# Differential attention: each softmax's head on its own 64 rows of TensorE, three part products, three score buffers

## Chip, core and metric

The kernel runs on one core of a Trainium2 chip. The metric is the device time of one execution in microseconds; before the change it is 2722.09 us, the median of three runs (2720.32 to 2725.2).

## What is computed

An encoder trunk of two layers on 1024 tokens of width 1024, in float32. Layer 0 mixes tokens by differential attention: for each of 8 heads, two softmaxes over all 1024 keys, with queries and keys of 64 dimensions each, are subtracted and applied to values of 128 dimensions. Layer 1 uses windowed grouped attention. Each layer has a gated MLP with a short convolution, and an input embedding gated by a sigmoid. Only the first layer's attention is changed:

```python
def one_block(qb):
    s = jnp.einsum('bqhd,bkhd->bhqk', qb, k).astype(jnp.float32) * scale
    pr = jax.nn.softmax(s, axis=-1).reshape(B, H, 2, DIFF_Q_BLOCK, S)
    a = (pr[:, :, 0] - lam_full * pr[:, :, 1]).astype(v.dtype)
    return jnp.einsum('bhqk,bkhe->bqhe', a, v)
```

## The kernel before

Most products run in a one-pass float32 format of reduced precision. An operand is therefore split into a high and a low part, and a product of two operands is a sum of part products. Queries and keys lie in scratch memory as 64 high rows and 64 low rows per softmax head.

The stage of differential attention is `diff_attn`. Its units are (head h, block qt of 128 queries), 64 in all. For one unit, `weights` does this for each of the two softmaxes a: four score products (L784, L785) into a score buffer of 128 x 1024 (two PSUM banks, S0 or S1); the negated row maximum on VectorE (L786); the exponential with its row sum on ACT (L790) into one of 11 buffers `e`. A stacked tile holds high parts on rows 0 to 63 and low parts on rows 64 to 127; `k2` is the same key tile with the halves exchanged. So one product with `k1` gives high x high + low x low, and one with `k2` the two mixed terms: all four part products in two products of 128 rows. Then a reciprocal on VectorE (L799), and two instructions on POOL (L801, L802) scale the second exponential and add it to the first, which frees the second buffer.

`values` follows two units later (LAG = 2): eight transposes (L813) into banks b4 and b5, copied out by ACT (L817) and VectorE (L819); eight float32 products with the values (L822, sixteen passes in the trace) into b2 or b3; a copy and a square with row sum on ACT (L826, L828), which read the sum. After every fourth unit, `subln_steps` normalises four blocks: small instructions on VectorE (L726) and POOL (L729), four scalings (L734), four transposes (L740, b2 or b3), an eviction on ACT (L743).

The order of instructions on each engine isn't that of the code: a scheduler in the framework fills each engine's list by a timeline of its own when the program is built, and semaphores for the tiles follow from it. On the chip each engine takes its list strictly from the front.

The next stage, the output projection, starts when the transposed heads `oT` are there.

Of the kernel before, what the change touches and what calls it, by code (L numbers as in the profile page):

```python
# [7 lines left out]
F32 = mybir.dt.float32  # L8
F32R = mybir.dt.float32r
# [4 lines left out]
PSUM = bass.MemoryType.PSUM  # L14
DRAM = bass.MemoryType.DRAM

P = 128
S = 1024
D = 1024
KT = D // P  # L20
HS = 512
# [32 lines left out]
def f32(ap):  # L54
    return ap.bitcast(F32)
# [55 lines left out]
END_BANKS = ["b2", "b3"]  # L111
P_BANKS = ["b0", "b1", "b4", "b5", "b6", "b7"]
DOWN_BANKS = ["b0", "b1", "b2", "b4", "b6", "b7", "b3", "b5"]
MIX_BANKS = ["b4", "b2", "b5", "b3"]


class Trunk:
# [603 lines left out]
    def subln_steps(self, h, hf, st, psum):  # L721

        nc = self.nc
        on, ss, z2 = st
        c = slice(hf * 4, hf * 4 + 4)
# [12 lines left out]
        tp = self.bank(psum, END_BANKS)  # L738
# [9 lines left out]
    def diff_attn(self, ap, psum, side):  # L748
        nc = self.nc
        v = nc.vector  # L750
        self.oT = [None] * NH
        ld, outs = {}, {}

        def load(h):
            b, hh = h // 2, 2 * (h % 2)
            qq, k1, k2 = (
                ap.at(f"{n}{h % 2}", [P, 2, S], F32R, self.nm("stk")) for n in ("q", "k", "l")
            )
            self.stack(k1[:], self.ks[b][:], slice(hh, hh + 2))
            self.stack(qq[:], self.qs[b][:], slice(hh, hh + 2))  # L760
            self.stack(k2[:], self.ks[b][:], slice(hh, hh + 2), swap=True)
            vt = ap.pools["v"].tile([P, 8, P], F32, tag="v", bufs=2, name=self.nm("v"))
            nc.sync.dma_start(vt[:], self.vs[:, :, h * P : (h + 1) * P])
            ld[h] = (qq, k1, k2, vt)
# [7 lines left out]
        def weights(h, qt):  # L772
# [3 lines left out]
            qq, k1, k2, _ = ld[h]  # L776
            sm = self.cp.tile([P, 8], F32, tag="sm", bufs=8, name=self.nm("sm"))
            es = []
            for a in range(2):
                ps = psum.at(f"S{a}", [P, S], F32, self.nm("S"))  # L780
                q_ = qq[:, a, qt * P : (qt + 1) * P]
                for kb in range(2):
                    sl = slice(kb * HS, (kb + 1) * HS)
                    nc.tensor.matmul(ps[:, sl], q_, k1[:, a, sl], start=True, stop=False)  # L784
                    nc.tensor.matmul(ps[:, sl], q_, k2[:, a, sl], start=False, stop=True)  # L785
# [19 lines left out]
        def values(h, qt, ea):  # L805

            vt = ld[h][3]
            at = ap.pools["a"].tile([P, 8, P], F32, tag="a", bufs=ABUF, name=self.nm("aT"))
            for kh in range(2):
                tp = psum.at(f"b{4 + kh}", [P, 4, P], F32, self.nm("T"))  # L810
# [9 lines left out]
            acc = self.bank(psum, END_BANKS)  # L820
# [738 lines left out]
    def run(self, out):  # L1559
# [41 lines left out]
        with ExitStack() as c:  # L1601
            ap = self.attn_pools(c, "a0", ["k0", "q0", "l0", "v", "a", "k1", "q1", "l1", "e"])
            psum = Bank(c, self.tc, "ps_a0", ["S0", "b2", "b3", "b4", "b5", "S1"], PSUM)
            self.diff_attn(ap, psum, [])
# [76 lines left out]
```

## Time and profile before

| What | Value |
|---|---|
| median of three runs | 2722.09 us |
| profiled execution | 2722.41 us |
| its span | 2720.6 us |
| TensorE (PE) busy | 2631.9 us, 97% |
| VectorE (DVE) busy | 1935.3 us, 71% |
| ScalarE (ACT) busy | 1185.5 us, 44% |
| GpSimd (POOL) busy | 1109.1 us, 41% |
| mean granted TensorE clock | 0.991 |

A matmul's duration in the trace includes its way through the pipeline; how fast matmuls follow each other is read from their starts. PEld are the weight loads that lie beside them. A name such as `S<-stk,stk` is output and inputs.

### The profile page before, as it was taken

How to read it: one execution, taken by the hardware profiler on the slowest of the kernel's cores; microseconds unless marked ns; L12 is line 12 of the kernel's file. 1: busy time of each engine (PE TensorE's matmuls, PEld its weight loads, DVE VectorE, ACT ScalarE, POOL GpSimd, SP SyncE). 2: the span in 40 equal slices, each digit the busy share in tenths (PEclk: the TensorE clock that was granted, in tenths of full speed). 3: DMA queues.
4: the chain of work that ended last, by engine and by line, in shares of the span. 5: the costliest groups of instructions: out<-in, count | busy, mean ns of one | idle time of the engine just before them, and what ended most of it. 6: DMA issues, size and time to landing. Idle time of an engine off the chain costs nothing. (4 is left out here: it accounts for less than half of the span.)

```text
span 2720.6 us, 33379 instructions
## 1 busy us (share of the span) xinstructions
PE 2631.9 (97%) x12670; PEld 2187.4 (80%) x12670; DVE 1935.3 (71%) x2250; ACT 1185.5 (44%) x2090; POOL 1109.1 (41%) x625
## 2 busy tenths in 40 slices
PE   7999999999999999999999999999999999999998
PEld 6888888888788888878888788878778888788877
DVE  7650588884798888866677556873988888856664
ACT  5322577773444444441134326872544444421142
POOL 2642577774233434325312353442343444334211
PEclk9999999999999999999999999999999999999999
DMA  6443623302423232244314347104322223344122
GB/s 245 157 152 124 186 65 109 101 9 99 142 69 93 70 93 75 88 147 144 108 46 146 110 166 247 48 1 147 117 78 85 89 74 93 128 135 139 62 70 93
DMA packets 204133, 296.24 MB, mean 109 GB/s; under 512 B 9524, under 2 KB 138693, under 8 KB 200261
## 3 DMA queue, kind: packets, MB, share of 16 engines
q1 hardware_dynamic: 203349, 293.72, 33.2%
q8 instruction: 100, 1.64, 0.2%
q14 instruction: 60, 0.49, 0.1%
q10 hardware_dynamic: 624, 0.39, 0.1%
HBM read 207.83 MB, written 86.25 MB: 108 GB/s over the span
## 5 line engine op out<-in xcount | busy, mean ns | idle before, releaser
L152 POOL TENSOR_TENSOR wl<-wr,wh 128x1024 fp32r<-128x1024 f32 (+1 forms) x113 | 296.5, 2640 | 490.1 <-ACT wh L146 386.8
L1150 POOL TENSOR_TENSOR sf<-wr 128x1024 f32<-128x1024 f32 x44 | 146.9, 3338 | 503.1 <-DVE w L1160 503.1
L1325 DVE TENSOR_TENSOR res<-res,ps 128x512 f32<-128x512 f32 x320 | 216.8, 684 | 147.7 <-PE ps L245 145.0
L241 PE MATMUL ps<-gh,wh 128*128 128x512 f32 x704 | 275.4, 391 | 4.2 <-DVE ug L1266 3.2
L244 PE MATMUL ps<-gl,wh 128*128 128x512 f32 x704 | 275.1, 391 | 1.0 <-DVE gl L152 1.0
L245 PE MATMUL ps<-gh,wl 128*128 128x512 f32 x704 | 274.8, 390 | 0.0
L241 PE MATMUL ps<-hn,wh 128*128 128x512 f32 x544 | 215.2, 396 | 2.8 <-DVE gt L1423 1.9
L245 PE MATMUL ps<-hn,wl 128*128 128x512 f32 x544 | 213.5, 393 | 0.6 <-DVE wl L152 0.6
L244 PE MATMUL ps<-hn,wh 128*128 128x512 f32 x544 | 213.9, 393 | 0.0
L146 ACT CAST wh<-wr 128x1024 fp32r<-128x1024 f32 (+1 forms) x140 | 144.8, 1092 | 143.6 <-PE ps L244 95.8
L790 ACT ACTIVATE e<-S,sm 128x1024 f32<-128x1024 f32 x128 | 142.2, 1113 | 86.1 <-DVE sm L786 84.0
L146 ACT CAST gh<-gr 128x1024 fp32r<-128x1024 f32 x44 | 46.2, 1049 | 292.1 <-PE ps L245 213.3
L1159 ACT CAST w<-sf 128x1024 fp32r<-128x1024 f32 x88 | 92.7, 1053 | 184.4 <-PE ps L1188 108.9
L786 DVE TENSOR_REDUCE sm<-S 128x1 f32<-128x1024 f32 x128 | 152.2, 1216 | 17.1 <-PE S L785 15.6
L241 PEld LDWEIGHTS ps<-gh,wh 128*128 128x128 f32 x704 | 132.8, 189 | 32.7 <-ACT wh L146 3.5
L244 PEld LDWEIGHTS ps<-gl,wh 128*128 128x128 f32 x704 | 132.8, 189 | 29.2 <-DVE gl L152 1.7
L245 PEld LDWEIGHTS ps<-gh,wl 128*128 128x128 f32 x704 | 132.7, 189 | 27.7
L802 POOL TENSOR_TENSOR e<-e,e 128x1024 f32<-128x1024 f32 x64 | 152.0, 2375 | 5.2
L1186 PE MATMUL ps<-qb,w 128*128 128x512 f32 x352 | 137.3, 390 | 3.5 <-DVE uv L1262 3.5
L1186 PE MATMUL ps<-qa,w 128*128 128x512 f32 x352 | 136.7, 389 | 2.0 <-ACT w L1159 2.0
L1187 PE MATMUL ps<-qa,w 128*128 128x512 f32 x352 | 137.1, 389 | 0.0
L1187 PE MATMUL ps<-qb,w 128*128 128x512 f32 x352 | 137.0, 389 | 0.0
(256 smaller groups left out, 7255.2 us busy)
## 6 DMA issues: line engine op xcount, KB each, us to landing
wr<-ffn_w_up SPq DMA_DIRECT2D x88, 512.0 KB, 5.3
gs<-c SPq DMA_DIRECT2D x44, 512.0 KB, 3.0
wr<-ffn_w_down SPq DMA_DIRECT2D x22, 1024.0 KB, 5.1
gr<-gs SPq DMA_DIRECT2D x44, 512.0 KB, 4.3
qs<-rhl SPq DMA_DIRECT2D x32, 512.0 KB, 3.2
wr<-diff_w_qkv SPq DMA_DIRECT2D x12, 1024.0 KB, 5.8
ks<-rhl SPq DMA_DIRECT2D x20, 512.0 KB, 3.1
spill<-res SPq DMA_DIRECT2D x16, 512.0 KB, 3.0
```

What stands on the lines that cost most here:

```text
L146: self.nc.scalar.copy(out, in_)
L152: self.marks[eng] = eng.tensor_tensor(out, in_, f32(hi), op=ALU.subtract)
L241: ins = self.nc.tensor.matmul(out, ah, bh, start=first, stop=False)
L244: self.nc.tensor.matmul(out, ah, bl, start=False, stop=False)
L245: self.nc.tensor.matmul(out, al, bh, start=False, stop=last)
L786: v.tensor_reduce(sm[:, a : a + 1], ps[:], axis=AX.X, op=ALU.max, negate=True)
L790: nc.scalar.activation(e[:], ps[:], AF.Exp, bias=sm[:, a : a + 1], accum_out=sm[:, 2 + a : 3 + a])
L802: nc.gpsimd.tensor_tensor(ea[:], ea[:], eb[:], op=ALU.add)
L1150: eng.tensor_tensor(sf[:, 0:2], v[:, 2].unsqueeze(1).to_broadcast([P, 2, HS]), v[:, 0::3], op=ALU.add)
L1186: mm(ps, ah, bh, start=first and i == 0, stop=False, skip_group_check=True)
L1187: mm(ps, ah, bl, start=False, stop=False, skip_group_check=True)
L1325: v.tensor_tensor(self.res[dt][:, sl], self.res[dt][:, sl], acc[:], op=ALU.add)
```

## The change

The two softmaxes of a head now lie beside each other on the rows: the first on rows 0 to 63, the second on rows 64 to 127, for queries and for keys, with high and low parts behind each other in a partition. A score is the sum of three part products (high x high, high x low, low x high) of 64 rows each; low x low is left out. The code issues them in pairs, one for each softmax. The exchanged key tile and its loads are gone. There are three score buffers in turn (S0, S1, S2, six banks), and the banks b6 and b7 in turn hold all other tiles of the stage: transposes, value sums, and the transposes of `subln_steps`. In the program, each score product of 64 rows carries a tile size of 64 x 128 and the row position 0 or 64.

```diff
--- before.py
+++ after.py
@@ -111,6 +111,7 @@
 END_BANKS = ["b2", "b3"]
 P_BANKS = ["b0", "b1", "b4", "b5", "b6", "b7"]
 DOWN_BANKS = ["b0", "b1", "b2", "b4", "b6", "b7", "b3", "b5"]
+PAIR_BANKS = ["b6", "b7"]
 MIX_BANKS = ["b4", "b2", "b5", "b3"]
 
 
@@ -735,7 +736,7 @@
                 on[:, qt, :], on[:, qt, :], ss[:, qt : qt + 1], None, op0=ALU.mult
             )
         yield
-        tp = self.bank(psum, END_BANKS)
+        tp = self.bank(psum, PAIR_BANKS)
         for i in range(4):
             nc.tensor.transpose(
                 tp[:, i * P : (i + 1) * P], on[:, hf * 4 + i, :], self.ident
@@ -749,19 +750,20 @@
         nc = self.nc
         v = nc.vector
         self.oT = [None] * NH
-        ld, outs = {}, {}
+        ld, outs, turn = {}, {}, [0]
 
         def load(h):
             b, hh = h // 2, 2 * (h % 2)
-            qq, k1, k2 = (
-                ap.at(f"{n}{h % 2}", [P, 2, S], F32R, self.nm("stk")) for n in ("q", "k", "l")
-            )
-            self.stack(k1[:], self.ks[b][:], slice(hh, hh + 2))
-            self.stack(qq[:], self.qs[b][:], slice(hh, hh + 2))
-            self.stack(k2[:], self.ks[b][:], slice(hh, hh + 2), swap=True)
+            kk, qq = (ap.at(f"{n}{h % 2}", [P, 2, S], F32R, self.nm("stk")) for n in ("k", "q"))
+            for t, src in ((kk, self.ks[b]), (qq, self.qs[b])):
+                v_ = src[:].rearrange("(e r h) s -> r e h s", e=2, h=4)
+                for a in range(2):
+                    nc.sync.dma_start(
+                        f32(t[a * 64 : (a + 1) * 64]), v_[:, :, hh + a, :]
+                    )
             vt = ap.pools["v"].tile([P, 8, P], F32, tag="v", bufs=2, name=self.nm("v"))
             nc.sync.dma_start(vt[:], self.vs[:, :, h * P : (h + 1) * P])
-            ld[h] = (qq, k1, k2, vt)
+            ld[h] = (qq, kk, vt)
             self.rows_tile(self.oT, h, "oT")
             outs[h] = (
                 ap.pools["a"].tile([P, 8, P], F32, tag="o", bufs=2, name=self.nm("on")),
@@ -773,16 +775,24 @@
 
             if qt == 0:
                 load(h)
-            qq, k1, k2, _ = ld[h]
+            qq, kk, _ = ld[h]
             sm = self.cp.tile([P, 8], F32, tag="sm", bufs=8, name=self.nm("sm"))
+            qc = slice(qt * P, (qt + 1) * P)
+            ss = []
+            for _ in range(2):
+                ss.append(psum.at(f"S{turn[0] % 3}", [P, S], F32, self.nm("S")))
+                turn[0] += 1
+            for kb in range(2):
+                sl = slice(kb * HS, (kb + 1) * HS)
+                for i, (eq, ek) in enumerate(((0, 0), (0, 1), (1, 0))):
+                    for a in range(2):
+                        r = slice(a * 64, (a + 1) * 64)
+                        nc.tensor.matmul(
+                            ss[a][:, sl], qq[r, eq, qc], kk[r, ek, sl],
+                            start=(i == 0), stop=(i == 2),
+                        )
             es = []
-            for a in range(2):
-                ps = psum.at(f"S{a}", [P, S], F32, self.nm("S"))
-                q_ = qq[:, a, qt * P : (qt + 1) * P]
-                for kb in range(2):
-                    sl = slice(kb * HS, (kb + 1) * HS)
-                    nc.tensor.matmul(ps[:, sl], q_, k1[:, a, sl], start=True, stop=False)
-                    nc.tensor.matmul(ps[:, sl], q_, k2[:, a, sl], start=False, stop=True)
+            for a, ps in enumerate(ss):
                 v.tensor_reduce(
                     sm[:, a : a + 1], ps[:], axis=AX.X, op=ALU.max, negate=True
                 )
@@ -804,10 +814,10 @@
 
         def values(h, qt, ea):
 
-            vt = ld[h][3]
+            vt = ld[h][2]
             at = ap.pools["a"].tile([P, 8, P], F32, tag="a", bufs=ABUF, name=self.nm("aT"))
             for kh in range(2):
-                tp = psum.at(f"b{4 + kh}", [P, 4, P], F32, self.nm("T"))
+                tp = psum.cycle(PAIR_BANKS, [P, 4, P], F32, self.nm("T"))
                 for i in range(4):
                     kt = kh * 4 + i
                     nc.tensor.transpose(
@@ -817,7 +827,7 @@
                     nc.scalar.copy(at[:, 0:4], tp[:])
                 else:
                     v.tensor_copy(at[:, 4:8], tp[:])
-            acc = self.bank(psum, END_BANKS)
+            acc = self.bank(psum, PAIR_BANKS)
             for k in range(8):
                 nc.tensor.matmul(
                     acc[:, :P], at[:, k, :], vt[:, k, :], start=(k == 0), stop=(k == 7)
@@ -1599,8 +1609,8 @@
                 self.x_squares(i, tp.tile([P, D], F32, tag="t", name=self.nm("xsq")))
             self.qkv0(hn, self.xrcol, hp, tp, psum)
         with ExitStack() as c:
-            ap = self.attn_pools(c, "a0", ["k0", "q0", "l0", "v", "a", "k1", "q1", "l1", "e"])
-            psum = Bank(c, self.tc, "ps_a0", ["S0", "b2", "b3", "b4", "b5", "S1"], PSUM)
+            ap = self.attn_pools(c, "a0", ["k0", "q0", "v", "a", "k1", "q1", "e"])
+            psum = Bank(c, self.tc, "ps_a0", ["S0", "S1", "S2", "b6", "b7"], PSUM)
             self.diff_attn(ap, psum, [])
         gs = self.projected(0, io["diff_w_o"][0], pp[0])
         with ExitStack() as sc:
```

The scheduler places the work anew. At the start of the stage, on TensorE, before (S_251 and S_253 are the two softmaxes of unit 0, S_256 the first of unit 1):

```order
L784 MATMUL S_253_2204<-stk_243_2183,stk_242_2182 128x512
L785 MATMUL S_253_2204<-stk_244_2184,stk_242_2182 128x512
L784 MATMUL S_253_2204<-stk_243_2183,stk_242_2182 128x512
L785 MATMUL S_253_2204<-stk_244_2184,stk_242_2182 128x512
L784 MATMUL S_256_2218<-stk_243_2183,stk_242_2182 128x512
L785 MATMUL S_256_2218<-stk_244_2184,stk_242_2182 128x512
L784 MATMUL S_256_2218<-stk_243_2183,stk_242_2182 128x512
```

and now (S_250 and S_251 are the two softmaxes of unit 0, S_255 and S_256 those of unit 1, S_260 and S_261 of unit 2):

```order
L790 MATMUL S_250_2186<-stk_242_2173,stk_243_2174 128x512
L790 MATMUL S_251_2187<-stk_242_2173,stk_243_2174 128x512
L790 MATMUL S_250_2186<-stk_242_2173,stk_243_2174 128x512
L790 MATMUL S_251_2187<-stk_242_2173,stk_243_2174 128x512
L790 MATMUL S_255_2212<-stk_242_2173,stk_243_2174 128x512 x6
L790 MATMUL S_256_2213<-stk_242_2173,stk_243_2174 128x512 x6
L790 MATMUL S_260_2238<-stk_242_2173,stk_243_2174 128x512 x6
L790 MATMUL S_261_2239<-stk_242_2173,stk_243_2174 128x512 x6
L790 MATMUL S_270_2289<-stk_242_2173,stk_243_2174 128x512 x6
```

In unit 0 the products of the two softmaxes alternate, as in the code; from unit 1 on, all six of one softmax stand together, and all six of the other behind them.

In the middle of the stage, on TensorE, before (T_665 and T_666 are the transposes of unit 36, S_660 and S_662 the two softmaxes of unit 38):

```order
L784 MATMUL S_660_4081<-stk_592_3773,stk_591_3772 128x512
L785 MATMUL S_660_4081<-stk_593_3774,stk_591_3772 128x512
L784 MATMUL S_660_4081<-stk_592_3773,stk_591_3772 128x512
L785 MATMUL S_660_4081<-stk_593_3774,stk_591_3772 128x512
L822 MATMUL ps_657_4066<-v_594_3779,aT_654_4053 128x128 x8
L813 MATMUL T_665_4103<-identr_172,e_641_3991 128x128 x4
L813 MATMUL T_666_4109<-identr_172,e_641_3991 128x128 x4
L784 MATMUL S_662_4089<-stk_592_3773,stk_591_3772 128x512
L785 MATMUL S_662_4089<-stk_593_3774,stk_591_3772 128x512
L784 MATMUL S_662_4089<-stk_592_3773,stk_591_3772 128x512
L785 MATMUL S_662_4089<-stk_593_3774,stk_591_3772 128x512
```

and now (T_660 and T_661 are the transposes of unit 36, ps_662 its value sum, T_670 and T_671 are those of unit 37, S_743 and S_744 the softmaxes of unit 46, S_753 and S_754 of unit 47):

```order
L832 MATMUL ps_652_4204<-v_589_3893,aT_649_4191 128x128 x4
L790 MATMUL S_743_4662<-stk_675_4330,stk_676_4331 128x512 x6
L790 MATMUL S_744_4663<-stk_675_4330,stk_676_4331 128x512 x6
L832 MATMUL ps_652_4204<-v_589_3893,aT_649_4191 128x128 x4
L823 MATMUL T_660_4245<-identr_172,e_637_4130 128x128 x4
L823 MATMUL T_661_4251<-identr_172,e_637_4130 128x128 x4
L832 MATMUL ps_662_4257<-v_589_3893,aT_659_4244 128x128 x8
L823 MATMUL T_670_4300<-identr_172,e_647_4181 128x128 x4
L790 MATMUL S_753_4717<-stk_675_4330,stk_676_4331 128x512 x6
L790 MATMUL S_754_4718<-stk_675_4330,stk_676_4331 128x512 x6
L823 MATMUL T_671_4306<-identr_172,e_647_4181 128x128 x4
```

Scores were two to three units ahead of the transposes; now they are nine to ten units ahead, and the groups of six stand singly or in twos between transposes and values. The transposes and values of unit 36 follow each other with no score between.

On ACT at the same place, before (e_661 and e_663 are the exponentials of unit 38):

```order
L790 ACTIVATE e_661_4087,sm_659_4080<-S_660_4081,sm_659_4080 128x1024
L826 COPY on_595_3781<-ps_657_4066 128x128
L828 ACTIVATE jk_658_4076,ss_596_3782<-ps_657_4066 128x128
L817 COPY aT_664_4102<-T_665_4103 128x512
L795 ACTIVATE sm_659_4080<-sm_659_4080,neglam_193 128x1
L796 ACTIVATE z2_597_3783<-sm_659_4080 128x1
L790 ACTIVATE e_663_4095,sm_659_4080<-S_662_4089,sm_659_4080 128x1024
L790 ACTIVATE e_671_4138,sm_669_4131<-S_670_4132,sm_669_4131 128x1024
```

and now (e_745 and e_746 are the exponentials of unit 46; jk_663 is the square of unit 36's value sum, aT_669 the copy of unit 37's transposes):

```order
L800 ACTIVATE e_745_4677,sm_742_4661<-S_743_4662,sm_742_4661 128x1024
L836 COPY on_590_3895<-ps_662_4257 128x128
L838 ACTIVATE jk_663_4267,ss_591_3896<-ps_662_4257 128x128
L805 ACTIVATE sm_742_4661<-sm_742_4661,neglam_193 128x1
L806 ACTIVATE z2_680_4340<-sm_742_4661 128x1
L827 COPY aT_669_4299<-T_670_4300 128x512
L800 ACTIVATE e_746_4680,sm_742_4661<-S_744_4663,sm_742_4661 128x1024
L800 ACTIVATE e_755_4732,sm_752_4716<-S_753_4717,sm_752_4716 128x1024
```

The kinds of instruction between a unit's two exponentials are the same, but they now belong to units nine to ten earlier. e_746 waits in the program for POOL's addition of unit 45, whose second buffer it takes over, and T_661 for the square of unit 35.

## Rows read from the trace of the kernel before

**Rows 1.** The page's busy table: engine, busy us (share of the span), instructions.

```profile
PE 2631.9 (97%) x12670; PEld 2187.4 (80%) x12670; DVE 1935.3 (71%) x2250; ACT 1185.5 (44%) x2090; POOL 1109.1 (41%) x625
```

**Rows 2.** Table of stretches, one stretch of the stage.

```profile
core 0: us, PE busy (x) PEld busy (x) DVE busy (x) ACT busy (x) POOL busy (x), PEclk, DMA share, GB/s
340.00:380.00 40.00, 37.78 (x263) 33.30 (x262) 32.41 (x43) 28.73 (x81) 30.48 (x18) 1.00 0.29 89
```

**Rows 3.** Source view of line 784, the score products.

```profile
L784 PE MATMUL S<-stk,stk x256: 387/397/795, 295.1 to 613.4; 128*128 128x512 f32 x128
...
  ACT e L790: 50.5, 61
```

**Rows 4.** Timeline of PE, one steady unit: start, us, engine, line, operation, tiles.

```profile
561.34 1.04 PE L813 MATMUL T<-identr,e 128*128 128x128 f32 x8
562.13 0.47 PE L784 MATMUL S<-stk,stk 128*128 128x512 f32 x1
562.45 0.39 PE L785 MATMUL S<-stk,stk 128*128 128x512 f32 x1
...
563.84 0.39 PE L785 MATMUL S<-stk,stk 128*128 128x512 f32 x1
564.06 1.95 PE L822 MATMUL ps<-v,aT 128*128 128x128 f32 x16
565.85 1.04 PE L813 MATMUL T<-identr,e 128*128 128x128 f32 x8
```

**Rows 5.** Timeline of PE, later in the same four units.

```profile
574.45 0.60 PE L740 MATMUL ps<-identr,on 128*128 128x128 f32 x4
...
581.59 1.04 PE L813 MATMUL T<-identr,e 128*128 128x128 f32 x8
```

**Rows 6.** Timeline of PE, two small transposes between products.

```profile
125.67 0.39 PE L244 MATMUL ps<-hn,wh 128*128 128x512 f32 x1
125.91 0.24 PE L288 MATMUL ps<-identr,rows 88*128 88x88 f32 x1
...
126.25 0.40 PE L241 MATMUL ps<-hn,wh 128*128 128x512 f32 x1
...
131.96 0.39 PE L244 MATMUL ps<-hn,wh 128*128 128x512 f32 x1
132.28 0.25 PE L288 MATMUL ps<-identr,rows 33*128 33x33 f32 x1
...
132.79 0.40 PE L241 MATMUL ps<-hn,wh 128*128 128x512 f32 x1
```

**Rows 7.** Timeline, from a second exponential to POOL's addition.

```profile
559.75 1.11 ACT L790 ACTIVATE e<-S,sm 128x1024 f32<-128x1024 f32 x1
...
560.98 0.16 DVE L799 RECIPROCAL sm<-sm 128x1 f32<-128x1 f32 x1
...
562.54 2.39 POOL L802 TENSOR_TENSOR e<-e,e 128x1024 f32<-128x1024 f32 x1
```

**Rows 8.** Timeline, a subln instruction on DVE beside POOL's addition.

```profile
567.46 2.37 POOL L802 TENSOR_TENSOR e<-e,e 128x1024 f32<-128x1024 f32 x1
567.53 2.31 DVE L726 SCALAR_TENSOR_TENSOR ss<-ss,z 128x4 f32<-128x4 f32 x1
```

**Rows 9.** Timeline, transposes and values with no score product between.

```profile
626.24 1.03 PE L813 MATMUL T<-identr,e 128*128 128x128 f32 x8
...
626.54 0.20 ACT L828 ACTIVATION_READ_ACCUMULATOR jk<-ps 128x1 f32 x1
...
627.51 1.16 PE L822 MATMUL ps<-v,aT 128*128 128x128 f32 x8 [0.24 <-ACT aT L817]
```

**Rows 10.** Timeline of PE early in the stage.

```profile
301.05 0.63 PE L785 MATMUL S<-stk,stk 128*128 128x512 f32 x1
301.48 0.63 PE L784 MATMUL S<-stk,stk 128*128 128x512 f32 x1
```

**Rows 11.** Table of stretches around them.

```profile
300.40:304.00 3.60, 3.05 (x7) 1.99 (x7) 2.58 (x4) 1.66 (x6) 3.13 (x2) 0.51 1.08 377
```

## The prediction

> **What bounds the kernel now.** I read the busy table of the page first: TensorE 97% [rows 1]. An average over stages says little about this change, so the next view is the table of stretches, for the one stage that the change touches: between 340 and 380 us TensorE is busy 37.8 of 40 us, VectorE 32.4, ACT 28.7, POOL 30.5 [rows 2]. The stage runs from the first score product at 295.1 us to the last at 613.4 [rows 3], 64 units (head, block of 128 queries), so one unit costs 318.3 / 63 = 5.05 us. In the timeline one unit is to be seen whole: eight score products from 562.13 to 564.06, sixteen value products to 565.85, and eight transposes, whose stretch (561.34 to 562.13) is 0.79 us. From one batch of transposes to the next that is 4.51 us without a gap [rows 4]. Four units take 581.59 - 561.34 = 20.25 us [rows 4, 5], 5.06 each; every fourth unit holds four more transposes (574.45) [rows 5], half of 0.79 us, 0.10 a unit. So TensorE's own work is 4.61 us of 5.06, and it waits 0.45 a unit, 29 us in the stage, above all for the exponential that frees a score buffer [rows 3]. TensorE sets the pace here; the others have 19 to 28% to spare.
>
> **The change, part by part.**
>
> *Score products.* A unit had 8 of 128 rows; it now has 12 of 64 rows. From 562.45 to 563.84 six of them start 0.23 us apart, and over the eight the step is 0.228 [rows 4]. Written as pairs, one on rows 0 to 63 and one on rows 64 to 127, twelve could run in six steps. The order of the changed program decides whether they do: only the first unit of 64 keeps the pairs. In each of the other 63 all six products of one softmax stand first and all six of the other behind them, in 30 units directly, in 33 with other work between (the pieces of TensorE's order in the section on the change). TensorE starts products in the order in which they stand; six neighbours on the same 64 rows cannot share a step. No row shows a score product of 64 rows, but a transpose with 33 rows lasts 0.25 us and one with 88 rows 0.24 [rows 6]: fewer rows make it no shorter, so I take 0.228 for 64 rows too. The other end, half of that, is a pair in one step (rival C). 256 products more x 0.228 = +58.4 us. The first unit's pairs can save six steps, -1.4. Where two groups on different rows stand next to each other (30 times a before b, 5 times b before the next a), the second's first can run beside the first's last if the array takes two at once: between 0 and 35 x 0.228 = 8; no row shows it, and I take the middle, -4.
>
> *Changing between 64 and 128 rows.* Each group of score products now stands between products on all 128 rows. I count 184 such borders in the order, 92 trips in and out. Before has a place of the same kind: a transpose with 33 rows, which uses a 64-row tile. From the product ahead of it at 131.96 to the second one behind it at 132.79 pass 0.83 us; the same three instructions with an 88-row transpose, on the full array, take 126.25 - 125.67 = 0.58 [rows 6]. A trip costs 0.25 us, though the narrower transpose has fewer columns. 92 x 0.25 = +23 us if nothing hides it; 0 if every trip falls into a wait that is there anyway. I take 23, since rows 6 are the nearest. The Trainium skill states the same as a rule that speaks against this change: "TensorEngine Tiling (Array Packing)", Key Properties, says that a change of tiling mode, not of the tile alone, drains the engine. By that rule alone the sum has a term above 0 here, and rows 6 agree with 0.25 us.
>
> *Two banks for everything else.* Three score buffers take six banks, so transposes, value sums and the four late transposes share b6 and b7. A second half of transposes now waits until the square on ACT has read the value sum of the unit before. Near the end of before, two units follow each other with hardly a score between: transposes start at 626.24 and take 0.79 us, but values start at 627.51, behind ACT's copy and its squares [rows 4, 9]: 0.48 us of wait, and with the new wait for the bank (the squares run until 626.74, and the first half would be done at 626.64) about 0.85. The order has this sequence, two batches of transposes and then the values with no score between, 10 times among the scores and 10 times behind them, because scores now run ten units ahead and the last ten units have none left: 20 x 0.85 = 17 us. Half a value group can also wait for VectorE: the copy of its transposes stands behind the small subln instruction, which lasts 2.31 us because it ends with POOL's addition (569.84 against 569.83) [rows 8]; 16 times, up to 1.4 us; I take 0.6, 10 us. Together 27 us of waits.
>
> *The third score buffer.* It can remove the wait for the exponential, in TensorE's 29 us. But where TensorE has 12 products in a unit the exponentials come round less often anyway. I let all of the 29 go and the 27 come: -2. The bounds are -20 (few of the new waits, since scores cover them) and +45 (next rival).
>
> *Loads.* One head loads four pieces of 512 KB in place of 3 MB, far ahead; nothing waited for them in the stage [rows 3], and nothing is gained. The removed buffers shift later stages' order a little: 0, with 10 either way.
>
> Sum: 58.4 - 1.4 - 4 + 23 - 2 = +74 us. The profiled execution took 2722.41 us (span 2720.6), within 0.4 of the median 2722.09, so the forecast is 2722 + 74 = 2796 us. A unit then needs 4.61 + 0.91 + 0.36 = 5.88 us of TensorE and waits about as long as before.
>
> **The rivals.**
>
> *A: the passes cost, the rest is covered.* Trips fall into waits, neighbouring groups overlap fully, and the third buffer takes 8 of the waits: 58.4 - 1.4 - 8 - 8 = +41, 2763 us. For it: 0.45 us of wait a unit is there to cover 0.36 of trips. Against it: waits for ACT and trips come at different borders.
>
> *B: the buffers of exponentials close a loop.* There are 11 such buffers, and with scores ten units ahead nearly all are held by units not yet transposed. The second exponential of a unit then needs the buffer that POOL frees at the end of the unit before: exponential at 559.75, reciprocal 560.98, addition done at 562.54 + 2.39 = 564.93 [rows 7], a loop of 5.2 to 5.3 us, 5.9 where one subln of 2.3 falls into each four units [rows 8]. That ties with TensorE's 5.88, and decides from half a microsecond more. With one exponential of 1.1 us queued ahead in ACT's order it is 7.0: from unit 17, where the lead reaches ten, 46 x (7.0 - 5.06) = 89, and 18 units x 0.8 = 14: +103, 2825 us.
>
> *C: the pairs do run together (other side).* If the array runs products on the two halves side by side although they stand six and six, 12 products take 6 steps, 1.37 us against 1.82: 64 x 0.455 = -29, with trips +23 and waits as in the sum, -2: 2714 us. It is a gain only if a pair takes under (1.82 - 0.36) / 1.37 = 1.07 steps. For it: nothing in rows; all products of before but three small transposes use 128 rows. Against it: products in the timeline start one behind another in their order [rows 4]. The Trainium skill has both sides, "TensorE: Matmul & The Clock Gate", Part 3: small products at different row positions run concurrently, but matmuls start and end strictly in program order. By its first half alone the change gains, by the second only the first unit's pairs do. No run here shows either for two 64-row tiles.
>
> *D: the clock.* Early in the stage, after waits of TensorE, score products start 301.48 - 301.05 = 0.43 us apart, at a granted clock of 0.51, the lower level of 1.2 GHz [rows 10, 11]. If new waits did that throughout, 768 products would cost 0.2 more: over +150, 2870 us and more. Against it: 0.45 us of wait a unit left the clock alone between 340 and 380, at 1.00 [rows 2].
>
> **How the numbers follow.** Forecast 0.62, A 0.17, B 0.13, C 0.05, D 0.03. The forecast's own spread is +55 to +95. The range is to hold 8 in 10: from 2755 (A and a little) to 2838 (B and a little); C and D stay out. A measurement of this kernel tells 0.2%, 5 us, from no change. Only C makes it faster, 0.04; same 0.02, a mixture of C with new waits; slower 0.94.
>
> **What would show it.** In the profile after: the score line has 768 products, in groups of six 0.228 us apart, also in the second group of six; a four-unit period of about 24 to 25 us in place of 20.25; the stage's last score product near 650 us or earlier, with ten units of transposes and values behind it; gaps of some 0.1 us at each border of score groups. The first unit alone shows whether a pair shares a step. Rival B shows as ACT waiting for POOL's addition ahead of the second exponential. I am wrong if the second six start while the first six run, if products of 64 rows stand closer than 0.2 us, or if the difference arises in another stage.

## The result and the profile after

The changed kernel takes 2787.69 us (2787.06 to 2788.89, 4 runs) against 2721.2 for the kernel before on the same chip: ratio 1.0252, 95% interval 1.0237 to 1.0267. The forecast was 2796, in a range of 2755 to 2838.

The page's busy table and the score and exponential lines (busy us, mean ns | idle before, releaser), against [rows 1]:

```profile
PE 2704.3 (97%) x12926; PEld 2221.4 (80%) x12926; DVE 1898.4 (68%) x2250; ACT 1196.0 (43%) x2090; POOL 1107.4 (40%) x625
...
L790 PE MATMUL S<-stk,stk 64*128 64x512 f32 x768 | 182.5, 419 | 10.8 <-ACT e L800 10.8
...
L800 ACT ACTIVATE e<-S,sm 128x1024 f32<-128x1024 f32 x128 | 142.1, 1112 | 49.5 <-POOL e L812 23.2
```

TensorE is busy for 72 us more. The source view of the score line, against [rows 3]:

```profile
L790 PE MATMUL S<-stk,stk x768: 383/393/793, 295.7 to 654.8; 64*128 64x512 f32 x192
...
its engine sat idle before it (us, times) until:
  ACT e L800: 25.7, 32
  issue: 8.7, 52
```

There are 768 products; the last starts at 654.8 in place of 613.4. This view adds the idle time ahead of products (PE) and ahead of their weight loads (PEld), which lie beside each other, so its 25.7 us, and the 50.5 of [rows 3], count most waits twice. The products alone waited 10.8 us for exponentials (the page's line above). In before they waited 16.4 (TensorE's waits: us in total, times, longest):

```profile
PE S L784 <- ACT e L790: 16.4, 16, 2.2
```

Stretches (us, then busy us of each engine, granted clock, DMA share, GB/s), against [rows 2]:

```profile
312.00:316.00 4.00, 4.00 (x13) 2.95 (x14) 2.22 (x4) 1.59 (x4) 3.45 (x2) 0.50 0.13 26
...
500.00:540.00 40.00, 38.05 (x246) 30.48 (x245) 22.17 (x36) 25.30 (x70) 28.23 (x17) 1.00 0.30 67
660.00:700.00 40.00, 37.59 (x275) 32.75 (x274) 16.61 (x28) 19.16 (x56) 15.03 (x10) 1.00 0.01 2
```

TensorE still sets the pace; behind the last score, at 660 to 700, only transposes and values are left and ACT and VectorE idle for half the time. The timeline of PE, against [rows 4, 5]:

```profile
502.52 0.60 PE L823 MATMUL T<-identr,e 128*128 128x128 f32 x4
...
506.28 2.24 PE L790 MATMUL S<-stk,stk 64*128 64x512 f32 x12
508.45 0.66 PE L823 MATMUL T<-identr,e 128*128 128x128 f32 x4
...
513.89 1.65 PE L790 MATMUL S<-stk,stk 64*128 64x512 f32 x6
515.47 1.09 PE L823 MATMUL T<-identr,e 128*128 128x128 f32 x8
...
526.74 0.60 PE L823 MATMUL T<-identr,e 128*128 128x128 f32 x4
```

Four units take 24.22 us (502.52 to 526.74). Six products that stand alone take 515.47 - 513.89 = 1.58 us; twelve that stand as six and six take 508.45 - 506.28 = 2.17, not twice that. And where they stand as pairs, in the first unit, two have started within 0.05 us, four within 0.35:

```profile
295.75 0.50 PE L790 MATMUL S<-stk,stk 64*128 64x512 f32 x2
```

(a timeline of 295.70 to 295.80; the two starts lie 2 ns apart, the next two 0.33 us later, then 0.23 a pair).

Where the time went, by TensorE's starts in the stage: from each product's start to the next product's start, summed by the first one's kind, with the kernels of the next section that bear on it.

```
us            stage  scores  transposes  values  rest
before        334.8   138.4        69.4   114.0  13.0
after         398.7   180.0        73.2   135.5  10.0
e4 layout     355.0   139.2        62.9   137.7  15.2
e3 128 rows   385.1   190.4        66.5   120.3   7.9
e8 rows       354.7   154.8        68.2   123.7   8.0
e9 written    322.3   117.2        80.1   116.0   9.0
```

The stage carries the whole difference: the product that stands 8000 ahead of the last starts 69.4 us later than in before (998.4 against 929.0), the last one 65.6.

### The profile page after: what moved, and what is told of

Same layout as the page of the kernel before. It is cut to its first block, busy times and chain, and to the rows that moved or that the text cites. A ratio compares the mean times of both kernels' runs of the same rounds, so it can differ in the third digit from the quotient of the medians.

```text
span 2786.2 us, 33901 instructions
## 1 busy us (share of the span) xinstructions
PE 2704.3 (97%) x12926; PEld 2221.4 (80%) x12926; DVE 1898.4 (68%) x2250; ACT 1196.0 (43%) x2090; POOL 1107.4 (40%) x625
## 5 line engine op out<-in xcount | busy, mean ns | idle before, releaser
L790 PE MATMUL S<-stk,stk 64*128 64x512 f32 x768 | 182.5, 419 | 10.8 <-ACT e L800 10.8
L800 ACT ACTIVATE e<-S,sm 128x1024 f32<-128x1024 f32 x128 | 142.1, 1112 | 49.5 <-POOL e L812 23.2
L790 PEld LDWEIGHTS S<-stk,stk 64*128 64x128 f32 x768 | 121.6, 191 | 46.5 <-ACT e L800 15.0
L832 PEld LDWEIGHTS ps<-v,aT 128*128 128x128 f32 x1024 | 123.8, 193 | 22.5 <-issue 11.1
L832 PE MATMUL ps<-v,aT 128*128 128x128 f32 x1024 | 139.1, 284 | 2.5 <-DVE aT L829 2.0
```

The source lines that it names most:

```text
L790: nc.tensor.matmul(ss[a][:, sl], qq[r, eq, qc], kk[r, ek, sl], start=(i == 0), stop=(i == 2),)
L800: nc.scalar.activation(e[:], ps[:], AF.Exp, bias=sm[:, a : a + 1], accum_out=sm[:, 2 + a : 3 + a])
L832: nc.tensor.matmul(acc[:, :P], at[:, k, :], vt[:, k, :], start=(k == 0), stop=(k == 7))
```

## The experiments

| kernel | us (range) | ratio to before, 95% |
|---|---|---|
| e1 pairs together | 2885.72 (2884.33 to 2888.14) | 1.0616, 1.0593 to 1.0638 |
| e2 six, then six | 2889.57 (2887.16 to 2892.6) | 1.0629, 1.0606 to 1.0653 |
| e3 all 128 rows | 2773.85 (2770.37 to 2775.55) | 1.0205, 1.018 to 1.0231 |
| e4 layout alone | 2742.74 (2741.5 to 2744.48) | 1.0089, 1.0068 to 1.0111 |
| e5 written order | 2746.28 (2744.77 to 2750.89) | 1.0099, 1.008 to 1.0119 |
| e6 layout, short lead | 2758.34 (2744.64 to 2758.91) | 1.0129, 1.01 to 1.0158 |
| e7 after, short lead | 2836.57 (2833.78 to 2842.41) | 1.0434, 1.0408 to 1.0459 |
| e8 rows alone | 2746.15 (2744.85 to 2746.55) | 1.0095, 1.0078 to 1.0113 |
| e9 banks turned | 2718.34 (2714.08 to 2721.97) | 0.9992, 0.9983 to 1.0000 |
| e10 the same, eight products | 2718.92 (2711.71 to 2723.54) | 0.9996, 0.9985 to 1.0008 |
| e11 neighbours | 2842.18 (2837.69 to 2844.87) | 1.0451, 1.0436 to 1.0465 |
| e12 banks turned, LAG 2 | 2718.78 (2716.56 to 2723.06) | 1.0000, 0.999 to 1.001 |

### Do pairs share a step? (e1, e2)

Both chain the score products one behind the other (`kept`), e1 in pairs, e2 as six and six.

```diff
-                    for a in range(2):
+                    for a in (1, 0):
...
+                        self.kept(
```

```diff
-            for kb in range(2):
...
-                    for a in range(2):
...
+            for a in (1, 0):
+                r = slice(a * 64, (a + 1) * 64)
+                for kb in range(2):
...
+                        self.kept(
```

> The changed kernel with the pairs held together: each unit's twelve score products are chained in their order on TensorE (the second softmax's product first in each pair, since its buffer comes free last), so that the two softmaxes alternate in nearly every unit; scores then run two to three units ahead and not ten. Theory 1 (the loss is the pairs that the order pulled apart): a pair takes one step of 0.23 us as in the first unit after the change, a unit needs 6 x 0.23 + 0.31 for the way into and out of the 64-row tiles + 0.80 + 1.79 + 0.10 = 4.4 us of TensorE, with 0.45 of waits 4.8 against 5.06 before: about 2705 us, 2690 to 2730. Rival (the loss is the shared banks and the borders between tile sizes): the pairs help little, 2760 us or more. Rival (the exponential chain of a unit, reduce, exponential, POOL, now bounds): 2730 to 2760.

> As the run with the pairs together, with nearly the same order of units, but inside a unit all six products of one softmax stand directly before all six of the other. If TensorE looks only a few products ahead, as the neighbouring groups of the changed kernel suggest (12 products in 2.16 us from start to the next instruction against some 1.6 for pairs), it costs 64 x 0.56 = 36 us more than the pairs. If it took no second product side by side at all: 64 x 1.37 = 88 us more. If order inside a unit doesn't matter: the same time as the pairs.

Timeline of PE in e1, one unit:

```profile
501.98 1.66 PE L791 MATMUL S<-stk,stk 64*128 64x512 f32 x12
503.57 1.09 PE L825 MATMUL T<-identr,e 128*128 128x128 f32 x8
504.90 1.16 PE L834 MATMUL ps<-v,aT 128*128 128x128 f32 x8 [0.24 <-ACT aT L829]
506.68 1.16 PE L834 MATMUL ps<-v,aT 128*128 128x128 f32 x8 [0.62 <-DVE aT L831]
```

Twelve products in 503.57 - 501.98 = 1.59 us: a pair shares a step. Yet the kernel is 98 us slower than after, and e2, whose twelve take 2.17, almost the same: 4 us apart, where 36 were expected. TensorE is no longer the bound; e1's second rival names the chain that is, at a far smaller size (2730 to 2760). Both maxima now stand back to back on VectorE (timeline), and the first exponential waits for both:

```profile
503.68 2.35 DVE L798 TENSOR_REDUCE sm<-S 128x1 f32<-128x1024 f32 x2 [1.28 <-PE S L791]
505.95 0.68 DVE L831 COPY aT<-T 128x512 f32<-128x512 f32 x1
```

The copy of the transposes comes behind them, the values behind the copy, the next scores behind the exponential. TensorE's products waited 73.3 us for exponentials (17 times), 10.8 in after. Fifteen of the 17 come once in four units, 4.5 us each: there a subln scaling of 2.36 us stands on VectorE between the two maxima. The page's line, then VectorE and PE at one of them:

```profile
L791 PE MATMUL S<-stk,stk 64*128 64x512 f32 x768 | 132.8, 479 | 73.3 <-ACT e L802 73.3
```

```profile
610.44 1.22 DVE L798 TENSOR_REDUCE sm<-S 128x1 f32<-128x1024 f32 x1
611.61 2.36 DVE L735 TENSOR_SCALAR on<-on,ss 128x128 f32<-128x128 f32 x1
613.89 1.21 DVE L798 TENSOR_REDUCE sm<-S 128x1 f32<-128x1024 f32 x1
...
616.39 2.50 PE L791 MATMUL S<-stk,stk 64*128 64x512 f32 x10 [4.50 <-ACT e L802]
```

e2 has fifteen such waits of 3.9 us. Around each of them the granted clock is 0.50 for a few us (from 614.1 to 621.0 here), where after has 1.00 from 318.5 us on, so part of the 98 us is the clock. My reversed order of the two may add one maximum, about 1.2 us, to the chain; that is an estimate, and no run separates it.

### What the parts cost (e3, e4, e8)

e3 keeps TensorE's order of after, each product on all 128 rows (so it sums the other softmax's rows too). e4 is before with the change's three score buffers and two shared banks; e8 is after with before's two score buffers and four other banks.

```diff
-                            ss[a][:, sl], qq[r, eq, qc], kk[r, ek, sl],
+                            ss[a][:, sl], qq[:, eq, qc], kk[:, ek, sl],
```

```diff
-                ps = psum.at(f"S{a}", [P, S], F32, self.nm("S"))
+                ps = psum.at(f"S{turn[0] % 3}", [P, S], F32, self.nm("S"))
...
-            acc = self.bank(psum, END_BANKS)
+            acc = self.bank(psum, PAIR_BANKS)
```

```diff
-                ss.append(psum.at(f"S{turn[0] % 3}", [P, S], F32, self.nm("S")))
+                ss.append(psum.at(f"S{turn[0] % 2}", [P, S], F32, self.nm("S")))
...
-            acc = self.bank(psum, PAIR_BANKS)
+            acc = self.bank(psum, END_BANKS)
```

> The changed kernel with the same twelve score products in the same order on every engine, but each taken over all 128 rows (the scores are then sums over both softmaxes; only the time is of use): no 64-row tiles, so no change of tile size and nothing side by side. If a way in and out costs 0.31 us (92 of them, 28 us) and neighbouring groups gain 0.78 us by lying side by side (28 of them, 22 us, and 1.4 in the first unit), the two nearly cancel: 2783 us, about 5 below the changed kernel. If the borders cost nothing: 2810. If lying side by side gains nothing: 2758.

> The kernel before, with its eight products of 128 rows, its three key and query tiles and their loads, but with the change's PSUM layout: three score buffers in turn, b6 and b7 in turn for everything else. Theory 1: the layout is nearly neutral, new waits for the banks against the old ones for the score buffer, 2715 to 2735 us. Rival (the layout and the long lead that it lets the scores take are what costs): 2750 us or more.

> The changed kernel's twelve 64-row products a unit with the two score buffers and the four other banks of the kernel before. If the costs add (layout +24, four more products a unit +31, 64 rows +14), this one is before + 45: 2755 to 2770. Rival (with two buffers the scores of one half cannot start until the exponential of the same half is done, and the longer groups, 1.59 instead of 1.0 us, stand on that chain): 2785 or more, so that the third buffer was needed. Second rival (the layout's +24 and the products' +31 are the same wait): 2740 to 2750.

e3 lies between its ranges (2783 forecast, 2758 if overlap gains nothing), and so does e4 (up to 2735, or over 2750). From before one way: layout +24 (e4), twelve products in place of eight, in after's order and with its loads, +31 (e3), 64 rows +14 (after). The other way: rows alone +27 (e8), the layout on top +41 (after). The costs don't add: e8 came out 17 us under before + 45, in the range of its second rival, whose reason (the same wait in both) was not tested.

What 64 rows do, by e3's timeline beside after's, one group alone and one double:

```profile
509.99 1.64 PE L790 MATMUL S<-stk,stk 128*128 128x512 f32 x6
511.46 0.60 PE L823 MATMUL T<-identr,e 128*128 128x128 f32 x4
...
520.03 3.00 PE L790 MATMUL S<-stk,stk 128*128 128x512 f32 x12
522.87 0.60 PE L823 MATMUL T<-identr,e 128*128 128x128 f32 x4
```

Medians over the stage, with the gap ahead: alone 1.48 + 0.03 on 128 rows, 1.59 + 0.20 on 64, so a trip costs 0.28 us; double 2.86 + 0.03 against 2.17 + 0.20, so it saves 0.52. After has 62 alone and 28 double, 62 x 0.28 - 28 x 0.52 = +3. Of the other 11 of e3's 14 us some belongs to the clock: 0.50 at 312 to 316 in after, 1.00 in e3; the rest was not divided.

Why the layout costs, by e4's waits between 340 and 600 us (us in total, times, longest), ACT's and TensorE's, and last TensorE's in before:

```profile
ACT e L792 <- PE T L815: 29.5, 28, 1.7
...
PE S L786 <- ACT e L792: 14.8, 32, 0.9
PE ps L824 <- DVE aT L821: 5.9, 3, 3.5
PE ps L824 <- ACT aT L819: 2.4, 10, 0.2
...
PE S L784 <- ACT e L790: 12.7, 13, 1.0
```

The first exponential waits for a transpose that frees one of the 11 buffers, because scores run ten units ahead. But TensorE pays little for that: it waits 14.8 us for exponentials in place of 12.7. What is new is that its values wait for the copies of the transposes. By the starts over the whole stage, the time beyond the usual step from one product to the next is 62 us in e4 and 39 in before; of the 23 more, 3 stand ahead of scores at an exponential, 12 ahead of values at a copy, 4 ahead of transposes at the square that reads their bank last.

Between e8 and after it is the groups: e8 has 57 double and 10 alone, after 28 and 62. That is 57 x 2.17 + 10 x 1.59 = 140 us against 159, and 67 gaps of 0.2 against 90: 24 of the 41 us. Most of the rest, by the starts, are waits: 8 us of transposes for the square that reads their bank last (none in e8), 5 of scores for exponentials.

### Is it the lead? (e6, e7)

The first score product of a unit is chained behind the last value product of the unit three back, in e4's kernel and in after.

```diff
+                        if kb == 0 and i == 0 and a == 0:
+                            self.kept(ins)
...
+            self.kept(ins)
```

> The kernel before with three score buffers and two shared banks (the layout alone, +24 us), and in it the first score product of a unit chained behind the last value product of the unit three back, so that the scores cannot run ten units ahead. Theory 1 (the layout's cost is the run-ahead: the e buffers fill, the first exponential waits for a transposition that frees one, and the scores' end leaves 45 us of transpositions and values with nothing beside them): most of the 24 us comes back, 2718 to 2730. Rival (the cost is the two banks shared by transposed weights, outputs and turned outputs, whose copies TensorE waits for): the time stays at 2738 to 2750. Second rival (the short lead uncovers the chain from a maximum to the next scores, as in the two kernels with an order chained product by product): over 2760.

> The changed kernel, the first score product of a unit chained behind the last value product of the unit three back, and nothing else. Theory 1 (run-ahead costs): 10 to 25 us under the changed kernel, 2763 to 2778. Rival (the lead is what covers the chain from a maximum over its exponential to the next scores in the same buffer): 2800 to 2880, with TensorE waiting over 1 us for the exponential at the first score of a unit, as in the two kernels whose products were chained one by one (2886 and 2890).

No. e6 gave nothing back, and e7 lost 49 us more, in its rival's range: the lead covers more than it costs. In e7 a value product starts 0.82 us behind the score ahead of it (mean of 31; 0.35 in after), and a score 0.67 us behind the transpose ahead of it (31; 0.22 in after). e6's profile is of its one run at 2744.64; what the three near 2758 lost stays open.

### Is it the shared banks? (e11)

After with TensorE's order as it fell in e8: transposes, second six of a unit, first six of the next, values.

```diff
+                at = turned(eas.pop(k))
...
+                eb = half(*units[i - 1], 1, sms[i - 1])
...
+                eas[i] = half(*units[i], 0, sms[i])
...
+                values(*units[k], at)
```

> The changed kernel, TensorE's order alone written out as it fell in the kernel with twelve 64-row products and the old banks (2746): both groups of transpositions, second six products of a unit, first six of the next, value products. Only 28 of the changed kernel's groups of six stood in neighbouring pairs, 62 alone; there 57 pairs. Theory 1 (the 41 us between those two kernels are mostly the groups that stand alone, 0.23 us more each beside two trips of 0.2 us: about 24 us by the starts of the products): 2758 to 2772. Rival (it is the two banks that transposed weights, outputs and turned outputs share, whose readers TensorE waits for): 2780 to 2800, with waits at the transpositions.

60 doubles of 2.17 us, as wanted, and 2842: theory 1 is out for this order, and what the lone groups cost in after is not told by it. The rival has the right place and too small a size. Waits of PE at 340 to 600, and the timelines of ACT and PE at one of them:

```profile
PE T L821 <- ACT jk L844: 53.5, 38, 2.1
```

```profile
509.82 1.11 ACT L796 ACTIVATE e<-S,sm 128x1024 f32<-128x1024 f32 x1 [3.37 <-DVE sm L792]
...
511.40 1.11 ACT L796 ACTIVATE e<-S,sm 128x1024 f32<-128x1024 f32 x1 [0.38 <-DVE sm L792]
...
512.65 0.29 ACT L844 ACTIVATE jk<-ps 128x128 f32<-128x128 f32 x1
...
513.08 0.66 PE L821 MATMUL T<-identr,e 128*128 128x128 f32 x4 [2.10 <-ACT jk L844]
```

The value sum was complete at about 510.5, but its square, the bank's last reader, stands behind two exponentials in ACT's list; the second half of the transposes needs that bank and starts at 513.08. After waits only 1.5 us for that square between 340 and 600 (8 times). I take it that its loose order, with groups alone and a long lead, keeps TensorE clear of these two banks, so that the layout's price is paid as lone groups there and as waits here; e11 changes lead and order together, so this is argued and not shown.

### Can it be had without the price? (e5, e9, e10, e12)

e5 writes out TensorE's order (transposes of the unit three back, twelve in pairs, values), VectorE's copy ahead of the maxima, and lets the square read the copied output. e9 and e10 below keep the square so and write out ACT's order too.

```diff
-                junk[:], acc[:, :P], AF.Square, accum_out=ss[:, qt : qt + 1]
+                junk[:], on[:, qt, :], AF.Square, accum_out=ss[:, qt : qt + 1]
```

> The changed kernel with TensorE's order of this stage written out, unit by unit: the transpositions of the unit three back, then the twelve score products in pairs (one on each half of the rows), then the value products of the unit three back; VectorE takes the copy of the transposed weights ahead of the two maxima, and the Square reads the copied output instead of the bank. Theory 1 (the pairs cost 0.23 us each when both halves are ready, and what made the paired kernel slow was the chain maximum, exponential, next scores with too little other TensorE work beside it): a unit is 1.6 + 0.1 + 0.8 + 1.8 + 0.1 = 4.4 us of TensorE against a period of 5.06 before, and the chain from a score to the next score in the same buffer is about 4.4 us too, so 2695 to 2720, most likely 2710: at or under the kernel before. Rival (any order in which both scores stand together puts the two maxima, 2.4 us of VectorE, in a row on the path, whatever stands beside them): a period near 5.6 to 6.2 us a unit, 2790 to 2880. The trace tells: waits of TensorE at the first score of a unit under 0.4 us, or over 1 us.

2746 in place of 2710: TensorE waits at a bank again. Its waits at 340 to 600 us:

```profile
PE T L827 <- ACT on L848: 28.8, 47, 1.4
```

The copy of the value sum stands behind an exponential, and the second half of the transposes needs its bank. Neither theory had that wait. e9 turns the order, so that each bank rests for a stretch:

```diff
+            st = scores(*units[i]) if i < n else None
...
+                turn_half(k, eas[k], ats[k], 0)
+            ea = expo(st, 0) if st else None
...
+                values(k - 1, *units[k - 1], ats.pop(k - 1))
+            eb = expo(st, 1) if st else None
...
+                turn_half(k, eas.pop(k), ats[k], 1)
```

Both halves of the transposes of unit k use one bank, the values between them the other, and the next unit the reverse. e10 puts before's eight products into the same order; e12 is e9 with a shorter distance.

```diff
+                    self.kept(nc.tensor.matmul(ps[:, sl], q_, k1[:, a, sl], start=True, stop=False))
+                    self.kept(nc.tensor.matmul(ps[:, sl], q_, k2[:, a, sl], start=False, stop=True))
```

```diff
-LAG = 3
+LAG = 2
```

> The pinned and paired kernel again, with the order inside a unit turned so that no bank is wanted back at once: twelve score products in pairs, first four transpositions of the unit three back, the value products of the unit before that one in the other bank, second four transpositions; ScalarE's and VectorE's order written out to match. The pinned kernel of before lost 28.8 us in 340 to 600 us, in its second four transpositions, to the copy of the output that had left the same bank just before, which stood behind an exponential. Theory 1 (the pairs are worth their 0.23 us each, and only the waits for the two shared banks ate the gain): a unit of TensorE is 1.58 + 0.2 + 0.97 + 1.94 = 4.7 us, some 40 us of waits go, 2700 to 2715, under the kernel before. Rival (the chain maximum, exponential, next scores, 2.6 to 2.9 us beside 2.9 us of other products, takes the place of the bank's wait): 2725 to 2750, with TensorE waiting for an exponential at the first score of a unit.

> The same pinned order, banks and three score buffers, with the eight products on all 128 rows of the kernel before in place of the twelve paired ones: tells what the pairs are worth and what the written order is worth. A unit of TensorE is 1.87 + 0.97 + 1.94 = 4.78 us against 4.7 in pairs, without the two trips into 64-row tiles in that. Theory 1 (pairs and eight full products cost nearly the same, so any gain over the kernel before is the order's and the third buffer's): within 8 us of the paired one, 2700 to 2722. Rival (the pairs are the gain): 2725 to 2745.

> The paired kernel in the order with two banks turned about (2718), its transpositions two units behind the scores in place of three, so that three units of scores and not four stand at the stage's start with no other products beside them. There a unit took 5.49 us in place of 4.7 and TensorE's clock fell to half (0.50 to 0.56 of full at 304 to 316 us). Theory 1 (that start costs 2.5 us of wait and some 1.2 us of half clock a unit): 3 to 6 us less, 2712 to 2716, at last under the kernel before by more than the measurement can hide. Rival (GpSimd's two operations, some 8 us behind the scores, are then late for the transpositions): every unit waits, 2725 or more. Second rival (what the stage gains is lost in the stretch behind it, at 700 to 740 us, where TensorE waits for VectorE and its clock falls): 2717 to 2721.

Timeline of PE in e9, one unit and the start of the unit four further on, then its waits at 340 to 600:

```profile
515.05 1.66 PE L797 MATMUL S<-stk,stk 64*128 64x512 f32 x12
516.64 0.66 PE L840 MATMUL T<-identr,e 128*128 128x128 f32 x4
517.14 1.95 PE L853 MATMUL ps<-v,aT 128*128 128x128 f32 x16
518.92 0.60 PE L840 MATMUL T<-identr,e 128*128 128x128 f32 x4
519.45 1.66 PE L797 MATMUL S<-stk,stk 64*128 64x512 f32 x12
...
534.10 1.66 PE L797 MATMUL S<-stk,stk 64*128 64x512 f32 x12
```

```profile
PE S L797 <- ACT e L815: 5.7, 2, 2.9
PE ps L853 <- DVE aT L845: 0.3, 1, 0.3
```

This unit takes 4.40 us, where one without a gap took 4.51 in before [rows 4]; four units take 534.10 - 515.05 = 19.05 us against 20.25. The bank waits are gone, and the kernel is 69 us under after. e10 has e4's banks, buffers and products and is 24 us under e4: in this written order, with the square off the bank and LAG = 3, the layout costs nothing that can be measured. Yet e9 only equals before, and e10 equals it: theory 1 of e10 holds, the pairs are worth nothing beyond eight full products. A group costs 1.59 + 0.20 us against 1.92 + 0.03 in e10, 60 x 0.16 = 10 us saved. But the four units at the start, which have no other products beside them, take 19.4 us against 11.1. There TensorE waits 4.18, 2.56 and 2.56 us for exponentials (1.31, 0.61 and 0.60 in e10), and at half clock a group of twelve takes 2.7 to 2.9 us in place of 1.65:

```profile
308.00:312.00 4.00, 2.58 (x12) 1.81 (x12) 1.43 (x3) 2.62 (x6) 2.33 (x2) 0.50 1.11 318
```

e10 has 1.00 in the same stretch. Against before, the stage of e9 is 12.5 us shorter (table) but begins 3.2 us later, and the kernel's last product starts 0.4 us earlier: the other 9 us are lost behind the stage, and where was not followed. e12's start is shorter (three units, 13.3 us) and its median the same; its theory 1 fell. Its second rival gave the right range, but not by what it named: the wait of TensorE for VectorE that ends at 721.0 us lasts 5.3 us, and the same wait in before (until 723.4) also 5.3. No version beat both kernels by more than can be measured.

## Why the prediction was right, and where it was not

The side and the size came out (+66 against +74), the place is right, and so is the period (24.2 us for four units; 24 to 25 forecast). But two terms were wrong and cancelled: the products by 31 to 49 us too much, the layout by 26 to 43 too little, as one or the other is changed first (e4, e8). So the near total is luck. One of the prediction's own signs of being wrong came true, "if the second six start while the first six run".

- *Passes, neighbours, trips: 58.4 - 1.4 - 4 + 23 = +76; e8 measures +27, e3 and after on top of e4 +45.* The step that failed is "the second's first can run beside the first's last", with its bound of 8 us. The second six start when three of the first six have: in the double group at 506.28 the second's first starts 7 ns after the first's third, and then the two alternate, 0.11 to 0.12 us apart. A double costs 0.69 us less than on 128 rows, not 0.23. The other part is cover: e4's products wait for exponentials, copies and banks, and the longer groups of e3 fill part of that (values row 137.7 to 120.3 us, of which 17.8 at the border to scores). A slip in the sum: over the eight, [rows 4] give (564.06 - 562.13) / 8 = 0.241 us, not 0.228, which would make 58.4 into 61.7.
- *Trips: 0.25 us each from [rows 6].* Right: 0.28 for a group alone. The Trainium skill, "TensorEngine Tiling (Array Packing)", Key Properties, says that a change of tiling mode drains the engine; the trace agrees, with these 0.28 us.
- *Two shared banks and the third buffer: -2; the layout measures +24 alone, +41 beside twelve products.* I let all 29 us of the old wait go and put it down to exponentials above all; the products' wait for them was 16.4 us and fell to 10.8 (the 50.5 of [rows 3] count weight loads too). And I priced the banks as waits beside a fixed order. Much of their price is the order that the scheduler builds around them: beside twelve products, 24 us of 41 are lone groups, and written out (e9, e10) the order takes the price away. How the rest divides stays open.
- *First unit's pairs.* Right in kind (2 ns apart), and the twelve take 1.49 us; the wait of 2.84 us and the half clock that follow hide the gain.
- *Loads, later stages: 0.* 4 us came back behind the stage, inside the 10.
- *Rivals.* A is partly true (cover). B's sign is there, ACT waits 23.2 us for POOL's addition, but TensorE's own wait for exponentials went down (10.8 against 16.4), so this loop is not what cost the time. C's premise is true for pairs, and partly for six and six, so "starts products in the order in which they stand" was too strong; e9 shows what C leaves out, a start with long waits at half clock and a chain to feed. D happened between 301.5 and 318.5 us only, where the granted clock was 0.50. The Trainium skill, "TensorE: Matmul & The Clock Gate", Part 3, says that products on different rows overlap, which the trace shows, and that they start and end strictly in program order, which the double groups contradict: in that group the seventh of the twelve starts at 506.855, ahead of the fourth (507.078), and the product that signals the first softmax's end only at 507.543.

## What to carry to other kernels

Two products of 64 rows share a step only if they stand near each other (twelve take 1.59 us in pairs, 2.17 as six and six), and a trip into 64-row tiles costs 0.28 us, so three part products in pairs (1.59 + 0.20) hardly beat two products on the full array (1.92). When buffers are moved, look at which reader frees each bank and what stands ahead of that reader in its engine's list; turn the order so that a bank rests between two uses. And where a scheduler sets the order, a layout's price is read from the order it builds, not from the waits alone: the same layout cost 24 us in one order and none in another (e4, e10). A view of one source line can add the waits of an engine's products and of its weight loads; take the products alone.

## What the runs showed of the hardware

- Two 64-row products on different halves start 2 ns apart, and a pair takes 0.23 us, as long as one product on 128 rows.
- Of six and six, the second group's first starts 7 ns after the first group's third (median of 28); twelve take 2.17 us, between 1.59 (pairs) and 2.86 (128 rows).
- TensorE's granted clock fell to 0.50 (1.2 GHz) at the start of the stage in after, behind a wait of 2.84 us, and in e9, behind one of 4.18; in before it fell for a shorter time behind 2.23 [rows 10, 11]. In e3 (1.70) and at the start of e10 (1.31), with full rows, it stayed at 1.00; in e11, with 64 rows, it fell behind 1.22. But in e10 it fell at 607.2 too, on full rows, where TensorE was busy 1.54 of 4 us (604 to 608), and in e9 two later waits of 2.85, at 510 and 589, left it at 1.00: neither a single wait nor the rows alone decide.
